# Hymba layer on one core: a third pair of gate-up group 1 made as seven products, and the token sums of pair 6 moved ahead of those of pair 5

## The chip, the cores and the metric

The kernel runs on 1 core of one Trainium2 chip. The metric is device time in microseconds (us), from the start to the end of the program on that core. Of each kernel there are several timed runs and one execution under the hardware profiler. Engines are named as in the profile: PE multiplies matrices, PEld loads their weights, DVE and ACT do elementwise work, POOL here mostly issues DMAs that add to memory, SP issues the other DMAs.

## The reference, cut to what matters

The layer is a feed-forward block, a mixer (a gated recurrence beside windowed attention) and a second feed-forward block, on 256 tokens of width 2048, all in float32. The change touches the gate-up product of both feed-forward blocks:

```python
def swiglu(x, w_gate_up, w_down):
    gate, up = jnp.split(x @ w_gate_up, 2, axis=-1)
    return (jax.nn.silu(gate) * up) @ w_down

ff = swiglu(rms_norm(x, pre_norm_ffn1[layer]), w_ffn1_gate_up[layer], w_ffn1_down[layer])
x = x + 0.5 * rms_norm(ff, post_norm_ffn1[layer])
...
ff = swiglu(rms_norm(x, pre_norm_ffn2[layer]), w_ffn2_gate_up[layer], w_ffn2_down[layer])
```

Here `w_gate_up` has 2048 rows and 2 x 5632 columns.

## The kernel before, in words

**Precision.** Every float32 operand is kept as two parts, a rounded `h` (cast by ACT) and the rest `l` (subtracted by DVE, `split_act`, L175 to L177). Each product is three matmuls: high by high, high by low, low by high (`three`, L435 to L447; the matmul is L441).

**Tiling of gate-up.** The columns are worked in 11 groups (0 to 10) of 512 gate and 512 up columns. In a group the 2048 rows of weights are 8 pairs (0 to 7) of two 128-row blocks. For one pair, the 256 tokens (two halves) by two row blocks by two column blocks form a 2 x 2 by 2 x 2 block product into four result banks `c[m][n]`. There are two ways to do it:

- a **plain** pair (`plain`, L450): eight block products, 24 matmuls of 512 columns. Its weights, 128 x 2048, come in one raw tile and are split in two halves: per half one ACT cast and one DVE subtraction (`split_half`, L168).
- a **seven** pair (`products`, L485): seven block products of sums, 21 matmuls, some into four more banks `p`. Its left sides are sums of the token blocks (made once by `sums_in`, L1023). Its right sides are sums of weight blocks: `prepare` (L903) splits the first block b11 (a 128 x 512 cast and subtraction) and lets POOL issue a DMA that adds 512 KB of weights onto the raw tile (L910). Later `splits` (L917) makes two 128 x 512 sums on DVE (L924, L925) and three half splits instead of two.

**The end of a group.** `boundary` (L1111) folds the `p` banks into the `c` banks by one ACT copy (L1122) and eight DVE additions (L1123 to L1133). Between them in the text, and waiting for them by bank, stand the 24 matmuls of pair 7, sorted by bank: (0,0) wants L1123, (1,0) wants L1126, (0,1) wants L1130, (1,1) wants L1133. Then follow the splits of pair 0 of the next group, and `units` (L1043): the gating of the finished group, which `first_pairs` (L1137) runs between the first pairs of the next.

**Order of the work.** From L1175 the order on every engine is the one written out by hand (`manual_schedule`): `first_pairs` for pairs 0 and 1, `pair_ahead` (L1156) for pairs 2 to 5, each of which first splits the weights of pair u + 1, then issues the products of pair u, then makes the last half split of u + 1; then pair 6 and the boundary. An engine does its instructions strictly in that order. Five `h` and five `l` buffers for halves go round (L44, L45), so ACT can cast a half only when PE has done with the half five places before. Weights come in five raw tiles; when a raw tile has been split, SP issues the next load (`load_next`, L894) in the order of a list that `plan` (L879) makes: by group and pair, with seven pairs moved forward by `PREPARED`.

**Which pairs are seven.** `MIXED_IN` is (2, 4, 5, 6). Groups 2 to 10 do these four as seven; group 1 does (2, 4); group 0 none. The token sums of pairs 2 and 4 are made in group 0 (L1105); those of pairs 5 and 6 in group 1, in `pair_ahead`, after pairs 4 and 5 (L1167). In `begin` (L413) the set of seven pairs of a group is read off as those pairs whose token sums exist; it sets how many matmuls each bank is to see.

Of the kernel before, what the change touches and what calls it, by code (L numbers as in the profile page):

```python
# [37 lines left out]
def hymba_layer_kernel(  # L38
# [37 lines left out]
    def nm(s):  # L76
        uid[0] += 1
        return f"{s}_{uid[0]}"

    def pa():  # L80
        return psum.tile([P, 512], F32, tag="pa", name=nm("pa"))

    def pb():
        return psum.tile([P, 512], F32, tag="pb", name=nm("pb"))
# [90 lines left out]
    def split_act(hi, lo, src):  # L175
        nc.scalar.copy(hi, src)  # L176
        nc.vector.tensor_tensor(lo, src, hi.bitcast(F32), ALU.subtract)  # L177
# [154 lines left out]
    class LeadN:  # L332


        def __init__(self, w, c0, slot):
            self.w, self.c0, self.slot = w, c0, slot
# [56 lines left out]
    def sums_of(u, w):  # L393

        nc.vector.tensor_tensor(
            w[:, S3::2, :], u[:, 0, :].rearrange("p (m t) -> p m t", m=2), u[:, :, P:T], ALU.subtract
        )
        nc.vector.tensor_tensor(w[:, S2, :], w[:, S1, :], u[:, 0, 0:P], ALU.subtract)
        nc.vector.tensor_tensor(w[:, S4, :], u[:, 1, 0:P], w[:, S2, :], ALU.add)
        return w  # L400

    class Blocks:
# [5 lines left out]
        rooms = 4  # L408

        def __init__(self, tiles, sums):  # L410
            self.tiles, self.sums = tiles, sums

        def begin(self, order, c=None):  # L413

            self.order, self.pos, self.seen = order, 0, {}
            self.c = c or [[pa(), pa()], [pb(), pb()]]
            self.p = None
            self.mixed = {u for u in order if u in self.sums}
            at = [i for i, u in enumerate(order) if u in self.mixed]
            some = len(at)  # L420
            plain = len(order) - some
            self.after = at[-1] + 1 if at else len(order) - 1

            self.within = bool(at) and self.after >= len(order) - 2

            self.rest = 6 * (len(order) - self.after - 1)
            self.of = {}
            for i in range(4):
                self.of["p", i] = 3 * some
                self.of["c", i // 2, i % 2] = 6 * plain + (3 * some if i < 3 else 0)  # L430
# [414 lines left out]
    NG = DFF // 512  # L845
    NU = DFF // 256
    LATE = 8

    MIXED_IN = (2, 4, 5, 6)
    PREPARED = {2: -0.5, 4: 0.5, 5: 1.5, 6: 3.5}  # L850
    AWAY = 8
    MIXED = range(0, 20, 2)
# [5 lines left out]
    class Gated(Blocks):  # L858
# [6 lines left out]

        def group(self, g, c=None):
            self.g = g
            self.begin(range(KT // 2), c)
            if g:
                self.rest = 6 if g < NG - 1 else 0  # L870
# [7 lines left out]

        def plan(self):  # L879

            self.here = {g: MIXED_IN if g > 1 else MIXED_IN[:2] for g in range(1, NG)}
            wanted = []
            for g in range(1, NG):
                for u in range(KT // 2):
                    before = PREPARED[u] if u in self.here[g] else u
                    wanted.append((g * KT // 2 + before, g, u))
            self.wanted = [at[1:] for at in sorted(wanted)]
            self.raws, self.firsts, self.split_of = {}, {}, {}
            for pool, n in ((rawp, 3), (self.room, 2)):
                for _ in range(n):  # L890
                    raw = pool.tile([P, 2048], F32, tag="raw", name=nm("raw"), bufs=n)
                    self.load_next(raw)
# [88 lines left out]
    def ffn(gated, w_dn, post_gain, again, gain=None, lead=None, aside=None):  # L981

        with ExitStack() as st:
# [6 lines left out]
            hts, sums, away = [], {}, {}  # L990
            where_X_was = []

            def room_for(tag):
                return work.tile([P, 512], F32, tag=tag, name=nm(tag))
# [21 lines left out]
            def even(u):  # L1016

                x = gated.tiles[u].rearrange("p k i t -> p (k i) t")
                nc.vector.tensor_tensor(
                    x, x.bitcast(F32), R[:, None, :].to_broadcast([P, 4, T]), ALU.mult  # L1020
                )

            def sums_in(u):  # L1023
                x = gated.tiles[u].bitcast(F32)
                whole = room_for("z").rearrange("p (k t) -> p k t", k=2)
                nc.vector.tensor_tensor(whole, x[:, :, 0, :], x[:, :, 1, :], ALU.add)
                ws = sums_of(whole, room_for("s").rearrange("p (j t) -> p j t", j=4))
                apart = u == MIXED_IN[1]
                w = (gated.room if apart else work).tile(
                    [P, 4, 2, P], F32R, tag="sp", name=nm("xs"), bufs=1 if apart else 3  # L1030
                )
                split_act(w[:, :, 0, :], w[:, :, 1, :], ws)
                gated.sums[u] = w

            def put_away(u):
                away[u] = dram.tile([P, 1024], F32, tag=f"ht{u}", name=nm("away"))
                nc.sync.dma_start(away[u], hts[u].bitcast(F32).rearrange("p k i t -> p (k i t)"))
# [54 lines left out]
            def some(steps, n):  # L1092
                for _ in range(n):
                    next(steps)
# [3 lines left out]
            for u in range(gated.pos, KT // 2):  # L1098
# [4 lines left out]
                for done in {4: (0, 1, 2), 5: (3, 4), 6: (5, 6), 7: (7,)}.get(u, ()):  # L1103
                    even(done)
                    if done in MIXED_IN[:2]:  # L1105
                        sums_in(done)
# [30 lines left out]
            def first_pairs(g, waiting):  # L1137

                gated.group(g)
                some(waiting, 1)  # L1140
                gated.prepare(g, MIXED_IN[1])
                some(waiting, 1)
                ahead = gated.splits(g, 1)
                some(ahead, 2)
                gated.prepare(g, MIXED_IN[2])
                for one in gated.take(g, 0):
# [9 lines left out]
            def pair_ahead(g, u):  # L1156

                ahead = gated.splits(g, u + 1)
                next(ahead)
                if u + 1 == MIXED_IN[1]:  # L1160
                    gated.prepare(g, MIXED_IN[3])
                next(ahead)
                for one in gated.take(g, u):
                    one()
                for _ in ahead:
                    pass
                if g == 1 and u in (4, 5):  # L1167
                    sums_in(MIXED_IN[u - 2])
                if u == 5 and 1 < g <= AWAY // 2 + 1:
                    put_away(2 * g - 4)  # L1170
                    put_away(2 * g - 3)
# [3 lines left out]
            with tc.manual_schedule():  # L1175
                gated.prepare(1, MIXED_IN[0])
                some(gated.splits(1, 0), 2)
                for g in range(1, NG):
                    first_pairs(g, waiting)
                    for u in range(2, last - 1):  # L1180
                        pair_ahead(g, u)
                    if g < NG - 1:
                        ahead = gated.splits(g, last)
                        some(ahead, 2)
                        gated.prepare(g + 1, MIXED_IN[0])
                        for one in gated.take(g, last - 1):
                            one()
                        boundary(g)
                        waiting = units(gated.c, rest)
                        some(waiting, 2)  # L1190
# [185 lines left out]
    with ExitStack() as s2:  # L1376
# [227 lines left out]
        def gates(half):  # L1604

            sl = [pa(), pa()]
            for _ in proj_N_pieces(w_in, 4096 + half * 512, 512, xt, sl):
                side_step()
            g = mid.tile([P, 2, 512], F32, tag="g", name=nm("g"))
            for m in range(2):  # L1610
                by = rs2[:, m : m + 1]
                nc.scalar.activation(g[:, m, :], sl[m], AF.Sigmoid, scale=by)
                nc.vector.scalar_tensor_tensor(g[:, m, :], sl[m], by, g[:, m, :], ALU.mult, ALU.mult)
            return g
# [129 lines left out]
        for hp in range(4):  # L1744
            zf = headpair(2048 + hp * 256, "zf")
            if hp == 1:
                g = gates(0)
# [18 lines left out]
        g = gates(1)  # L1766
# [94 lines left out]
```

## Time and profile before

| | us |
|---|---|
| median of 3 runs (lowest to highest) | 1833.95 (1833.39 to 1834.18) |
| the profiled execution, its own time | 1832.88 |
| its span, first to last instruction | 1831.1 |
| PE busy in the span | 1814.2 (99%) |
| DVE busy in the span | 1627.3 (89%) |
| ACT busy in the span | 1129.4 (62%) |

The profiled execution lies 1.07 us below the median of the runs, and 1.78 us of its time lie outside the span. A busy PE is counted with modelled ends that overlap, so how dense the matmuls are is read from their starts. In rows of the timeline the first number is the start in us from the beginning of the span and the second the duration; a number in brackets is idle time just before, with what ended it. In rows of windows follow, for each engine, busy us and instructions.

### The profile page before, as it was taken

Reading aid. Unit: us, or ns where it says so; the run is one execution under the profiler, and the core shown is the slowest. Engines: PE = TensorE matmul, PEld = TensorE weight load, DVE = VectorE, ACT = ScalarE, POOL = GpSimd, SP = SyncE. Lnnn points to the kernel's source line nnn. Section 1 sums busy time; section 2 is a strip of 40 time slices with the busy share of each in tenths; the row PEclk is TensorE's granted clock in tenths of the full one; section 3 lists DMA queues with packets and bytes.
Section 4 is the critical chain, followed back from the end, with each engine's and each line's share of the span. In section 5 each row is a group of like instructions: output and inputs, shape, how many; then the busy total and the mean of one; then the engine's idle time right before and its main releaser. Section 6 shows DMA issues by size and latency. Waiting matters only on the chain.

```text
span 1831.1 us, 23305 instructions
## 1 busy us (share of the span) xinstructions
PE 1814.2 (99%) x8438; PEld 1504.0 (82%) x8438; DVE 1627.3 (89%) x2071; ACT 1129.4 (62%) x1492; POOL 114.4 (6%) x115
## 2 busy tenths in 40 slices
PE   9999999999999999999999999999999999999998
PEld 6888888888887888888888888788888888888886
DVE  7999999999999998477787798899999999999897
ACT  7565666665655666476587556556666666565563
POOL 1011111111000000000000000001111111000000
PEclk9999999999999999999999999999999999999999
DMA  8789999998665566555454456789998998855565
GB/s 301 230 234 283 278 280 253 251 266 241 249 226 197 195 253 216 203 175 178 165 173 150 161 208 249 223 243 267 280 277 267 252 251 251 268 218 207 193 231 185
DMA packets 200020, 422.42 MB, mean 231 GB/s; under 512 B 10984, under 2 KB 45888, under 8 KB 199136
## 3 DMA queue, kind: packets, MB, share of 16 engines
q1 hardware_dynamic: 178880, 380.95, 59.6%
q0 software_dynamic: 21024, 39.99, 12.7%
q8 instruction: 66, 1.08, 0.2%
q14 instruction: 50, 0.41, 0.1%
HBM read 408.29 MB, written 12.60 MB: 230 GB/s over the span
## 4 chain that ended last, share of the span: by engine, by line
PE 87%; DVE 5%; ACT 3%; DMA 3%; issue 2%; POOL 0%; SPq 0%; DVEq 0%; ACTq 0%; POOLq 0%
PE pa L441 37%; PE pb L441 33%; PE pa L309 5%; DVE l L177 3%; PE pa L314 3%; DMA raw<-in_w_ffn_gate_up_dram 2%; PE pa L364 2%; PE pa L362 2%; PE pa L363 2%; ACT h L176 1%; PE pa L1074 1%; PE pb L1074 1%; PE pb L1582 0%; PE pb L1556 0%; PE pb L1660 0%
## 5 line engine op out<-in xcount | busy, mean ns | idle before, releaser
L176 ACT CAST h<-raw 128x1024 fp32r<-128x1024 f32 (+1 forms) x861 | 846.9, 1013 | 448.6 <-PE pb L441 131.9
L177 DVE TENSOR_TENSOR l<-raw,h 128x1024 fp32r<-128x1024 f32 (+1 forms) x861 | 983.1, 1171 | 118.3 <-ACT h L176 83.8
L441 PE MATMUL pa<-h,xt 128*128 128x512 f32 x1104 | 387.2, 392 | 0.1
L441 PE MATMUL pb<-h,xt 128*128 128x512 f32 x952 | 339.7, 391 | 0.4 <-DVE pb L1126 0.4
L441 PEld LDWEIGHTS pa<-h,xt 128*128 128x128 f32 x1104 | 207.2, 188 | 43.9 <-DVE xt L232 0.6
L441 PE MATMUL pa<-l,xt 128*128 128x512 f32 x552 | 215.7, 391 | 0.2 <-DVE l L177 0.2
L441 PEld LDWEIGHTS pb<-h,xt 128*128 128x128 f32 x952 | 178.6, 188 | 43.2 <-DVE pb L1133 3.5
L441 PE MATMUL pb<-l,xt 128*128 128x512 f32 x476 | 185.6, 390 | 0.0
L441 PE MATMUL pb<-h,ht 128*128 128x512 f32 x464 | 163.8, 390 | 0.0
L441 PE MATMUL pa<-h,ht 128*128 128x512 f32 x464 | 163.7, 391 | 0.0
L910 POOL DMA_DIRECT2D raw<-in_w_ffn_gate_up_dram x76 | 92.0, 1211 | 737.0 <-DVE l L177 638.8
L309 PE MATMUL pa<-xt,h 128*128 128x512 f32 x512 | 124.5, 393 | 0.2 <-ACT h L176 0.2
L441 PEld LDWEIGHTS pa<-l,xt 128*128 128x128 f32 x552 | 103.7, 188 | 21.4 <-DVE l L177 1.4
L309 PEld LDWEIGHTS pa<-xt,h 128*128 128x128 f32 x512 | 93.8, 188 | 18.6 <-ACT h L176 0.6
L441 PE MATMUL pa<-h,xs 128*128 128x512 f32 x304 | 108.5, 389 | 0.0
L441 PE MATMUL pb<-h,xs 128*128 128x512 f32 x304 | 105.9, 389 | 0.0
L441 PEld LDWEIGHTS pb<-l,xt 128*128 128x128 f32 x476 | 89.4, 188 | 17.2
L441 PEld LDWEIGHTS pa<-h,ht 128*128 128x128 f32 x464 | 87.7, 189 | 18.4
L441 PEld LDWEIGHTS pb<-h,ht 128*128 128x128 f32 x464 | 87.3, 188 | 18.1
L441 PE MATMUL pa<-l,ht 128*128 128x512 f32 x232 | 90.9, 392 | 0.0
L441 PE MATMUL pb<-l,ht 128*128 128x512 f32 x232 | 90.5, 390 | 0.0
L314 PE MATMUL pa<-xt,l 128*128 128x256 f32 x512 | 69.1, 285 | 0.0
(289 smaller groups left out, 2516.9 us busy)
## 6 DMA issues: line engine op xcount, KB each, us to landing
raw<-in_w_ffn_gate_up_dram SPq DMA_DIRECT2D x350, 512.0 KB, 6.1
raw<-in_w_ffn_down_dram SPq DMA_DIRECT2D x88, 1024.0 KB, 5.3
raw<-in_w_mix_in_dram SPq DMA_DIRECT2D x52, 1024.0 KB, 4.9
raw<-in_w_ffn_gate_up_dram POOLq DMA_DIRECT2D x76, 512.0 KB, 8.8
raw<-in_w_mix_out_dram SPq DMA_DIRECT2D x16, 1024.0 KB, 5.0
away<-ht SPq DMA_DIRECT2D x16, 512.0 KB, 6.9
ht<-away SPq DMA_DIRECT2D x16, 512.0 KB, 7.8
pg<-in_post_norm_ffn_dram SPq DMA_DIRECT2D x4, 512.0 KB, 6.7
```

Of the source, the lines that this page charges most:

```text
L176: nc.scalar.copy(hi, src)
L177: nc.vector.tensor_tensor(lo, src, hi.bitcast(F32), ALU.subtract)
L309: nc.tensor.matmul(slot[f], weights(hs, kk, f), xcol(xt, k), start=(k == 0), stop=(k == KT - 1))
L314: nc.tensor.matmul(slot[f][:, 0:T], weights(ls, kk, f), xcol(xt, kh * 8 + kk, 0), start=False, stop=False,)
L362: nc.tensor.matmul(dst, xh, h[:, o : o + n], start=(k == 0), stop=False)
L363: nc.tensor.matmul(dst, xh, l[:, o : o + n], start=False, stop=False)
L364: nc.tensor.matmul(dst, xl, h[:, o : o + n], start=False, stop=(k == KT - 1))
L441: nc.tensor.matmul(self.bank(at), lhs, rhs, start=(n == 1), stop=n in (ends, self.of[at]), skip_group_check=n > ends,)
L910: nc.gpsimd.dma_start(raw[:, 0:1024].rearrange("p (k c) -> p k c", k=2), self.source(u, g)[:, :, 1], accum_op=ALU.add,)
L1074: nc.tensor.transpose(bank[:, o : o + P], zs[m][:, k * P : (k + 1) * P], ident)
```

## The change

Group 1 does three pairs as seven products, (2, 4, 6). For that the token sums of pair 6 are made after pair 3, and those of pair 5 (wanted from group 2 on) after pair 5, both in group 1. The set of seven pairs is now taken from the plan (`here`) and no longer from the sums that exist. In `plan`, pair 6 of group 1 is now placed at 3.5 by `PREPARED`, so its weights are loaded ahead of those of pair 5. Both feed-forward blocks run this code.

```diff
-            self.tiles, self.sums = tiles, sums
+            self.tiles, self.sums, self.summed = tiles, sums, sums
...
-            self.mixed = {u for u in order if u in self.sums}
+            self.mixed = {u for u in order if u in self.summed}
...
     MIXED_IN = (2, 4, 5, 6)
+    MIXED_FIRST = (2, 4, 6)
     PREPARED = {2: -0.5, 4: 0.5, 5: 1.5, 6: 3.5}
...
         def group(self, g, c=None):
             self.g = g
+            self.summed = self.here[g] if g else ()
             self.begin(range(KT // 2), c)
...
-            self.here = {g: MIXED_IN if g > 1 else MIXED_IN[:2] for g in range(1, NG)}
+            self.here = {g: MIXED_IN if g > 1 else MIXED_FIRST for g in range(1, NG)}
...
-                if g == 1 and u in (4, 5):
-                    sums_in(MIXED_IN[u - 2])
+                if g == 1 and u in (3, 5):
+                    sums_in(6 if u == 3 else 5)
```

## The prediction

> **What bounds the kernel now.** First the page, then the windows between the transposes of one group and the next, in both feed-forward blocks (group 1, then group 2, of each).
>
> ```profile
> PE 1814.2 (99%) x8438; PEld 1504.0 (82%) x8438; DVE 1627.3 (89%) x2071; ACT 1129.4 (62%) x1492; POOL 114.4 (6%) x115
> ```
>
> ```profile
> 62.51:106.19 43.68, 43.48 (x195) 35.58 (x194) 40.11 (x53) 24.80 (x30) 2.50 (x3) 1.00 0.79 240
> 106.19:147.99 41.80, 41.80 (x189) 34.50 (x188) 39.82 (x49) 26.18 (x30) 4.81 (x4) 1.00 0.93 276
> ...
> 1177.99:1223.07 45.08, 43.95 (x195) 35.66 (x195) 42.06 (x54) 24.64 (x30) 3.65 (x3) 1.00 0.71 213
> 1223.07:1264.86 41.79, 41.79 (x189) 34.47 (x188) 39.82 (x49) 26.21 (x30) 4.84 (x4) 1.00 0.93 275
> ```
>
> PE is the bound over the whole, but DVE is close behind: in group 2 it is busy 39.82 of 41.80 us. Group 1 shows PE short of its window, so there it waits. The PE timeline shows where: the starts of pair 6, of pair 7, of pair 7's banks (1,0) and (1,1), and of the next group, then the like in the second block.
>
> ```profile
> 89.24 0.39 PE L441 MATMUL pa<-h,xt 128*128 128x512 f32 x1
> ...
> 94.68 0.39 PE L441 MATMUL pa<-h,xt 128*128 128x512 f32 x1
> ...
> 96.41 0.50 PE L441 MATMUL pb<-h,xt 128*128 128x512 f32 x1 [0.20 <-DVE pb L1126]
> ...
> 99.29 0.46 PE L441 MATMUL pb<-h,xt 128*128 128x512 f32 x1
> ...
> 100.75 0.39 PE L441 MATMUL pa<-h,xt 128*128 128x512 f32 x1
> ```
>
> ```profile
> 1211.58 0.39 PE L441 MATMUL pa<-h,xt 128*128 128x512 f32 x1
> ...
> 1213.31 0.50 PE L441 MATMUL pb<-h,xt 128*128 128x512 f32 x1 [0.20 <-DVE pb L1126]
> ...
> 1216.18 0.48 PE L441 MATMUL pb<-h,xt 128*128 128x512 f32 x1
> ```
>
> Pair 6 is 24 matmuls in 94.68 - 89.24 = 5.44 us: 0.2267 us each. Bank (1,0) should start six matmuls after 94.68, at 96.04, and starts at 96.41, just after a fold addition. So at the end of group 1 DVE, not PE, already sets the pace. Now DVE around it:
>
> ```profile
> 93.54 0.69 DVE L1123 TENSOR_TENSOR pa<-pa,z 128x512 f32<-128x512 f32 x1
> ...
> 95.65 0.70 DVE L1126 TENSOR_TENSOR pb<-pb,z 128x512 f32<-128x512 f32 x1
> ...
> 98.50 0.70 DVE L1133 TENSOR_TENSOR pb<-pb,s 128x512 f32<-128x512 f32 x1
> ```
>
> ```profile
> 1210.44 0.69 DVE L1123 TENSOR_TENSOR pa<-pa,z 128x512 f32<-128x512 f32 x1
> ...
> 1215.40 0.70 DVE L1133 TENSOR_TENSOR pb<-pb,s 128x512 f32<-128x512 f32 x1
> ```
>
> The last fold addition ends at 98.50 + 0.70 = 99.20 and bank (1,1) starts at 99.29; in the second block 1216.10 and 1216.18. The end of group 1 is tied to L1133, and what is tied to L1133 is what I have to move.
>
> **What the change takes from PE.** Pair 6 goes from 24 to 21 matmuls: 3 x 0.2267 = 0.68 us in each block, 1.36 us in all. It is worth that only if DVE is no later.
>
> **What it adds to DVE, per block.** One subtraction for b11, two sums, one more half split. Their price is read start to start:
>
> ```profile
> 60.40 0.68 DVE L177 TENSOR_TENSOR l<-raw,h 128x512 fp32r<-128x512 f32 x1
> 61.00 0.74 DVE L1054 SCALAR_TENSOR_TENSOR s<-pb,scales,s 128x512 f32<-128x512 f32 x1
> ...
> 65.18 0.69 DVE L924 TENSOR_TENSOR raw<-raw 128x512 f32<-128x512 f32 x1
> 65.91 0.69 DVE L925 TENSOR_TENSOR raw<-raw 128x512 f32<-128x512 f32 x1
> 66.52 1.22 DVE L177 TENSOR_TENSOR l<-raw,h 128x1024 fp32r<-128x1024 f32 x1
> ...
> 69.84 4.62 DVE L177 TENSOR_TENSOR l<-raw,h 128x1024 fp32r<-128x1024 f32 x4
> 74.50 0.69 DVE L924 TENSOR_TENSOR raw<-raw 128x512 f32<-128x512 f32 x1
> ...
> 75.84 3.64 DVE L177 TENSOR_TENSOR l<-raw,h 128x1024 fp32r<-128x1024 f32 x3
> 80.37 1.22 DVE L177 TENSOR_TENSOR l<-raw,h 128x1024 fp32r<-128x1024 f32 x1 [0.90 <-ACT h L176]
> 81.51 0.68 DVE L1026 TENSOR_TENSOR z<-xt 128x512 f32<-128x512 f32 x1
> ...
> 83.99 0.69 DVE L177 TENSOR_TENSOR xs<-s,xs 128x512 fp32r<-128x512 f32 x1 [0.69 <-ACT xs L176]
> 84.95 2.36 DVE L177 TENSOR_TENSOR l<-raw,h 128x1024 fp32r<-128x1024 f32 x2 [0.26 <-ACT h L176]
> ```
>
> The subtraction takes 61.00 - 60.40 = 0.60 us. A half split takes (4.62 - 1.22) / 3 = 1.13. The two sums take 66.52 - 65.18 = 1.34, and the first starts 74.50 - (69.84 + 4 x 1.13) = 0.14 later than a dense queue would. Together 0.60 + 1.34 + 0.14 + 1.13 = 3.21 us.
>
> **What it moves.** The token sums hold DVE from 81.51 to 84.95, 3.44 us, of which 0.69 + 0.26 us wait for ACT, whose cast of the next half stands behind its cast of the sums. There are two such sets in group 1 before and after, so moving them adds nothing in itself. But the first set, and the new subtraction, now come ahead of the splits of pair 5, where DVE has its only idle time: 0.90 us at 80.37, and about 0.15 us inside the three halves from 75.84 (3.64 where three dense ones take 1.22 + 2 x 1.13 = 3.48). There it waited for a buffer that PE had not done with. That idle time is filled. In the second block it is less:
>
> ```profile
> 1193.29 3.64 DVE L177 TENSOR_TENSOR l<-raw,h 128x1024 fp32r<-128x1024 f32 x3
> 1197.28 1.23 DVE L177 TENSOR_TENSOR l<-raw,h 128x1024 fp32r<-128x1024 f32 x1 [0.35 <-ACT h L176]
> ```
>
> So the folds come later by 3.21 - 0.90 - 0.15 = **2.16 us** in the first block and by 3.21 - 0.35 - 0.15 = **2.71 us** in the second. L1133 then ends at 101.36 and 1218.81, the last bank of group 1 starts as much later, and what stands behind keeps its distance to L1133. Sum: 4.87 us. The 1.36 us of PE are not subtracted: PE only comes to the boundary earlier and waits longer. Groups 2 to 9 do not give it back, because PE runs through them without a gap (41.80 us each).
>
> **What lies beside.** ACT gets a 512-wide and a 1024-wide cast more; it is busy 24.80 of 43.68 us in group 1, so they cost nothing unless it falls behind DVE. The first half of pair 5, which ended at 75.84 + 3.64 = 79.48, comes later by 0.60 + 3.44 - 0.15 = 3.89 us and ends at 83.37; PE starts pair 5 at 89.24 - 5.44 = 83.80. That cover is 0.4 us; if it fails PE waits there instead, and the fold is no later. SP loads pair 6 one place sooner and pair 5 one place later, both freed before 65 us and wanted after 72. POOL issues one more adding DMA per block, behind nothing: between its issues lie tens of us.
>
> **A stall long enough to slow PE.** In the first block PE now reaches pair 7 at 94.68 - 0.68 = 94.00 and may start when L1123 ends, at 94.23 + 2.16 = 96.39, plus 0.06 (96.41 against the end of L1126 at 96.35): a stall of 2.45 us. In the second it is 1210.90 to 1213.90, 3.0 us. Before bank (1,0) come 0.6 us more. The trace shows what a like stall does:
>
> ```profile
> 558.20:561.62 3.42, 1.38 (x6) 0.91 (x6) 3.42 (x5) 3.02 (x4) 0.00 (x0) 1.00 0.00 0
> 561.62:565.03 3.41, 3.41 (x10) 2.63 (x9) 3.41 (x5) 1.58 (x2) 0.00 (x0) 0.50 0.91 317
> 565.03:568.44 3.41, 3.41 (x17) 2.81 (x16) 3.37 (x5) 2.11 (x2) 0.00 (x0) 1.00 0.75 300
> ...
> 1176.02:1179.43 3.41, 2.48 (x13) 1.68 (x12) 2.25 (x4) 2.63 (x4) 0.25 (x1) 1.00 0.09 36
> ```
>
> After 3.41 us with 6 matmuls the granted clock is 0.50 for 3.41 us, with 10 matmuls where 17 stand otherwise; after 3.41 us with 13 it stays 1.00. Six matmuls leave 3.41 - 6 x 0.2267 = 2.05 us idle. If such windows lie anywhere in time, a stall s holds 2.05 us of one with a chance of (3.41 + s - 4.10) / 3.41: 0.52 and 0.68. So one drop in the two blocks is likeliest, none about 0.15, two about 0.35. Its price: up to 7 x 0.2267 = 1.6 us, but bank (1,0) waits in any case, and the last bank waits for L1133. With the drop from 97.4 on, bank (1,0) starts at 98.56 and takes 6 x 0.45 us for most of its length, ending near 101.0 where it would be 100.0; the last bank starts near 102.3 and not at 101.45. That is 0.9 us; an earlier drop gives 0.5, a later one 1.4. I take 0.9.
>
> The Trainium skill, "TensorE: Matmul & The Clock Gate", section "Part 1: The HAM clock gate", has the clock fall to half after at least one idle window of about 3.4 us. By that rule neither stall would slow PE and the sum would be 4.87 us (rival 1). The trace disagrees in part: its drop at 561.62 came after a window with 6 matmuls in it.
>
> **Forecast.** The profiled execution would go from 1832.88 to 1832.88 + 4.87 + 0.9 = 1838.65; the median of the runs lies 1.07 higher, so 1839.7.
>
> **Rivals.**
> (1) Late folds, no drop of the clock: 1833.95 + 4.87 = 1838.8. It speaks for it that where between 6 and 13 matmuls the drop sets in isn't shown.
> (2) Faster: DVE isn't the bound, its queue between 75.84 and 93.54 being held back by buffers that PE frees. Then PE alone counts: 1.36 us less, and of the waits in group 1 (0.37 + 0.1 us per block) nearly all go: 1831.6. It decides if 3.21 + 0.68 = 3.9 us of what looks like DVE work were waiting; the rows show 1.05 and 0.50 us, and twice 0.95 for ACT. Against it speak too the two PE waits that DVE ends now.
> (3) Half of it: the 0.95 us behind each set of token sums shrink, because in the new places ACT is ahead. Up to 1.9 us per block less if all four go; with half gone 1839.7 - 1.9 - 0.9 = 1836.9. Against it: ACT's order is fixed, and its cast of the next half stays behind that of the sums.
> (4) Worse: the adding DMA is late.
>
> ```profile
> DMA to landing us min/median/max: 5.6/8.8/10.7
> ```
>
> It is issued when the new subtraction ends, near 76.5, and the first sum of pair 6 is due at 75.84 + 0.60 + 2 x 1.13 + 3.44 + 3 x 1.13 + 0.14 = 85.7. At the median it lands at 85.3, at the longest 1.5 us late: up to 3 us in both blocks, 1842.7.
> (5) Pair 6 stays plain: 1834. The plan, the loads and the bank counts all read the new tuple, so next to nothing.
>
> **Chances.** Forecast 0.58 (one or two drops: 1839.2 to 1841); rival 1 0.16; rival 2 0.06; rival 3 0.10; rival 4 0.10; rival 5 none worth a number. The range runs from 1836.7 to 1841.9: it takes in the forecast, rival 1, most of rival 3 and the nearer half of rival 4. A measurement here can tell about 0.2%, 3.7 us, from no change: slower 0.84 (forecast, 1, 4), same 0.10 (rival 3), faster 0.06.
>
> **What would show it.** Right: 8432 matmuls on PE; L1123 of group 1 near 93.54 + 2.16 = 95.7 in the first block and near 1210.44 + 2.16 + 2.71 = 1215.3 in the second (later by what a drop of the clock costs ahead of it); PE idle 2 to 3 us ahead of pair 7 of group 1, released by DVE; no DVE wait of 0.90 us ahead of pair 5; groups 2 to 9 at 41.80 us; a clock of 0.50 just behind one of the stalls, or none for rival 1. Wrong: a wait of DVE at L924 for a DMA (rival 4), or PE reaching pair 7 with DVE already there (rival 2).

## The result and the profile after

The changed kernel takes 1836.73 us (median of 22 runs, 1835.32 to 1839.15), the kernel before, timed beside it, 1832.89 us (22 runs, 1830.26 to 1834.63). The ratio is 1.0023, with a 95% interval of 1.0017 to 1.0029: **slower** by some 4.2 us (3.1 to 5.3).

Lines L1122 to L1133 of the kernel before are L1124 to L1135 in the changed one. First the page, then the windows of group 1 in both blocks (us, then busy us and instructions of PE, PEld, DVE, ACT and POOL, the granted clock, DMA share and GB/s).

```profile
PE 1813.9 (99%) x8432; PEld 1505.0 (82%) x8432; DVE 1633.8 (89%) x2079; ACT 1135.2 (62%) x1496; POOL 116.8 (6%) x117
```

```profile
63.41:109.29 45.88, 43.11 (x193) 34.88 (x191) 43.13 (x57) 26.40 (x32) 3.67 (x4) 1.00 0.83 239
...
1179.31:1227.86 48.55, 44.80 (x191) 36.31 (x192) 45.81 (x59) 26.14 (x32) 5.07 (x5) 0.96 0.76 209
```

PE has its six matmuls fewer. Group 1 went from 43.68 to 45.88 us and from 45.08 to 48.55 us. In the first block PE is busy no longer than before, and DVE is busy 3.0 us longer. Now PE around pair 7 of group 1: the last matmul of pair 6, then the first of the banks.

```profile
94.67 0.39 PE L441 MATMUL pa<-h,xs 128*128 128x512 f32 x1
97.36 0.50 PE L441 MATMUL pa<-h,xt 128*128 128x512 f32 x1 [2.30 <-DVE pa L1125]
...
99.48 0.50 PE L441 MATMUL pb<-h,xt 128*128 128x512 f32 x1 [0.47 <-DVE pb L1128]
...
102.37 0.46 PE L441 MATMUL pb<-h,xt 128*128 128x512 f32 x1
...
103.83 0.39 PE L441 MATMUL pa<-h,xt 128*128 128x512 f32 x1
```

```profile
1212.05 0.39 PE L441 MATMUL pa<-h,xs 128*128 128x512 f32 x1
1215.26 0.79 PE L441 MATMUL pa<-h,xt 128*128 128x512 f32 x1 [2.82 <-DVE pa L1125]
...
1217.98 0.63 PE L441 MATMUL pb<-h,xt 128*128 128x512 f32 x1
...
1221.05 0.39 PE L441 MATMUL pb<-h,xt 128*128 128x512 f32 x1
```

PE should go on 0.23 us after 94.67 and stands until 97.36: 2.46 us, and 2.98 us in the second block. What ends both stalls is the first fold addition. DVE in group 1 of the first block:

```profile
76.70 2.96 DVE L177 TENSOR_TENSOR l<-raw,h 128x512 fp32r<-128x512 f32 x3
79.58 0.68 DVE L1028 TENSOR_TENSOR z<-xt 128x512 f32<-128x512 f32 x1
...
83.01 3.50 DVE L177 TENSOR_TENSOR l<-raw,h 128x1024 fp32r<-128x1024 f32 x3 [0.26 <-ACT h L176]
86.54 0.69 DVE L926 TENSOR_TENSOR raw<-raw 128x512 f32<-128x512 f32 x1
...
87.87 2.50 DVE L177 TENSOR_TENSOR l<-raw,h 128x1024 fp32r<-128x1024 f32 x2
90.29 0.68 DVE L1028 TENSOR_TENSOR z<-xt 128x512 f32<-128x512 f32 x1
...
93.73 2.96 DVE L177 TENSOR_TENSOR l<-raw,h 128x1024 fp32r<-128x1024 f32 x3 [0.26 <-ACT h L176]
96.61 0.69 DVE L1125 TENSOR_TENSOR pa<-pa,z 128x512 f32<-128x512 f32 x1
...
101.58 0.70 DVE L1135 TENSOR_TENSOR pb<-pb,s 128x512 f32<-128x512 f32 x1
```

The token sums of pair 6 (L1028 at 79.58) stand where DVE waited 0.90 us before, and the wait is gone. From 76.70 on DVE's waits are the two for ACT inside each set of token sums, and some 0.15 us inside the two halves from 87.87 (2.50 us where two dense ones take 1.22 + 1.13 = 2.35). The first fold addition starts at 96.61; counted from the transposes of this group (63.41 here, 62.51 before) that is 95.71, where 93.54 stood: 2.17 us later. In the second block L1125 starts at 1214.52; this group began 1.32 us later than before, so it is 2.76 us later than 1210.44.

```profile
1214.52 0.69 DVE L1125 TENSOR_TENSOR pa<-pa,z 128x512 f32<-128x512 f32 x1
...
1219.48 0.70 DVE L1135 TENSOR_TENSOR pb<-pb,s 128x512 f32<-128x512 f32 x1
```

The clock in the 3.41 us windows around the two stalls:

```profile
95.71:99.12 3.41, 1.65 (x6) 1.05 (x6) 3.27 (x6) 1.83 (x2) 1.21 (x1) 1.00 0.75 219
99.12:102.53 3.41, 3.05 (x13) 2.30 (x14) 3.24 (x6) 0.82 (x2) 0.00 (x0) 1.00 1.04 210
1211.87:1215.28 3.41, 0.59 (x4) 0.17 (x2) 3.41 (x5) 3.41 (x5) 0.03 (x1) 1.00 0.41 96
1215.28:1218.69 3.41, 3.41 (x8) 2.73 (x9) 3.17 (x5) 0.16 (x1) 1.18 (x1) 0.50 0.98 288
```

The second stall was followed by a window at half the clock, the first was not. Groups 2 to 9 take 41.8 us each, as before.

### The profile page after: what moved, and what is told of

Same layout as the page of the kernel before. It is cut to its first block, busy times and chain, and to the rows that moved or that the text cites. A ratio compares the mean times of both kernels' runs of the same rounds, so it can differ in the third digit from the quotient of the medians.

```text
span 1834.7 us, 23314 instructions
## 1 busy us (share of the span) xinstructions
PE 1813.9 (99%) x8432; PEld 1505.0 (82%) x8432; DVE 1633.8 (89%) x2079; ACT 1135.2 (62%) x1496; POOL 116.8 (6%) x117
## 4 chain that ended last, share of the span: by engine, by line
PE 90%; DVE 5%; ACT 3%; DMA 1%; issue 1%; POOL 0%; DVEq 0%; SPq 0%; ACTq 0%; POOLq 0%
PE pa L441 39%; PE pb L441 34%; PE pa L309 5%; PE pa L314 3%; DVE l L177 2%; PE pa L364 2%; PE pa L363 2%; PE pa L362 2%; ACT h L176 1%; DMA raw<-in_w_ffn_down_dram 1%; PE pa L1076 1%; PE pb L1076 1%; DMA raw<-in_w_ffn_gate_up_dram 0%; PE pb L1584 0%; PE pb L1558 0%
```

## Experiments

**Theory**: the work queued on DVE in group 1 sets when the folds of that group end, PE waits for them, and a long enough wait halves PE's clock for a while. **Rivals**: the order of the token sums, the order of the loads, or the seven pair itself (its adding DMA, its bank order) does it. Later a second question came up: what is given back outside group 1.

**1. The order of the token sums alone.**

```diff
-    MIXED_FIRST = (2, 4, 6)
+    MIXED_FIRST = (2, 4)
```

> Group 1 keeps two seven pairs (2, 4); only the order of the token sums is new (pair 6 after pair 3, pair 5 after pair 5). Theory (DVE's queue sets when the folds of group 1 come, and the sums in their new place fill the idle time ahead of pair 5): the folds come 1.05 us sooner in the first block and 0.50 us in the second, PE waits 0.1 us or less at the boundary, and the time is 0.6 to 1.1 us below the kernel before. Rival (the moved sums delay pair 5 and cost by themselves): PE waits at pair 5 and the time is 1 us or more above the kernel before.

1831.1 us against 1832.18, ratio 0.9993 (0.9984 to 1.0002). Group 1 in the windows:

```profile
63.88:107.01 43.13, 43.13 (x196) 35.69 (x194) 40.15 (x53) 24.93 (x30) 2.51 (x3) 1.00 0.81 239
1177.28:1221.95 44.67, 43.74 (x194) 35.66 (x195) 41.99 (x55) 24.54 (x30) 3.65 (x3) 1.00 0.73 214
```

That is 0.55 and 0.41 us less than before; PE has no gap left in the first. The timing alone can't tell so little, the windows can. The moved sums cost nothing, they gain a little.

**2. Four seven pairs in group 1.**

```diff
-    MIXED_FIRST = (2, 4, 6)
+    MIXED_FIRST = (2, 4, 5, 6)
...
-                if g == 1 and u in (3, 5):
-                    sums_in(6 if u == 3 else 5)
+                if g == 1 and u in (3, 4):
+                    sums_in(5 if u == 3 else 6)
```

> Group 1 makes four pairs (2, 4, 5, 6) as seven products, the token sums of pair 5 after pair 3 and those of pair 6 after pair 4. Theory (DVE bound, no idle time left to fill): 3.21 us more per block than the changed kernel, less at most 0.3 us of small waits, so 6 to 6.4 us above it and 10.5 to 12 us above the kernel before, with PE stalls of about 6 us ahead of pair 7 and a clock of 0.50 after both. Rival (the loss of the change comes from the order or the loads, not from DVE work): 1.4 us less than the changed kernel, PE's 6 matmuls.

1840.81 us, ratio 1.0051 (1.0037 to 1.0065). The windows of group 1 are 49.31 and 51.15 us, together 6.0 us more than in the changed kernel (45.88 and 48.55): the theory, not the rival. But the stall came elsewhere, in pieces, and the total rose by only 4 to 5 us over the changed kernel (ratios 1.0051 and 1.0023 to 1.0026). PE's waits in the first block:

```profile
86.83 0.50 PE L441 MATMUL pa<-l,xs 128*128 128x512 f32 x1 [0.36 <-DVE l L177]
91.42 0.50 PE L441 MATMUL pa<-h,xt 128*128 128x512 f32 x1 [1.08 <-ACT h L176]
92.68 0.50 PE L441 MATMUL pa<-l,xt 128*128 128x512 f32 x1 [0.76 <-DVE l L177]
95.27 0.80 PE L441 MATMUL pa<-l,xs 128*128 128x512 f32 x1 [1.62 <-DVE l L177]
```

With so much queued on DVE, PE already waits for the splits of pairs 5 and 6, and the clock fell to 0.50 for 6.83 us in both blocks (in the second also for 3.41 us at the start of the group, from 1182.84).

**3. PE kept busy while it waits.**

```diff
+    zeros = stat.tile([P, 208], BF16, tag="line", name="line", bufs=1)
+    nc.vector.memset(zeros, 0.0)
...
+                if g == 1:
+                    for _ in range(25):
+                        nc.tensor.matmul(
+                            c[1][1][:, 0:208], zeros[:, 0:P], zeros, start=False, stop=True, skip_group_check=True
+                        )
                 bank(0, 0)
                 bank(1, 0)
```

> The changed kernel, with 25 matmuls of zeros (208 columns, added to the bank (1,1)) ahead of pair 7 of group 1, where PE otherwise stands still: the result is the same. Theory (a stall of 2.45 or 3.0 us makes the clock drop in more than half of the executions, 0.9 us each): no granted clock of 0.50 near either boundary, the folds as late as in the changed kernel, and a median 0.8 to 1.3 us below the changed kernel. Rival (the drop costs nothing, since the last bank waits for DVE anyway): the same time as the changed kernel within 0.3 us.

1836.03 us, ratio 1.0020 (1.0011 to 1.0028). The matmuls of zeros fill the stall:

```profile
94.78 0.39 PE L442 MATMUL pa<-h,xs 128*128 128x512 f32 x1
95.00 2.40 PE L1132 MATMUL pb<-line 128*128 128x208 bf16 x25
97.49 0.50 PE L442 MATMUL pa<-h,xt 128*128 128x512 f32 x1
```

The clock stayed at 1.00 in both blocks, and group 1 took 46.00 and 47.94 us: the cost without a drop. The times don't show the 0.8 to 1.3 us that were expected: this run lies 3.85 us above the kernel before that was timed beside it (1832.18), the changed kernel 3.84 us above its own in the result above and 3.96 in run 7 below, and the intervals of the ratios overlap. The windows show a part of it: both groups 1 together take 93.94 us, where the three profiled executions of the changed kernel (the result above, runs 7 and 8 below) took 94.43, 95.59 and 94.80.

**4. The token sums' additions on POOL.**

```diff
...
+                add = nc.gpsimd.tensor_tensor
+                add(t, x[:, :, 0, :], x[:, :, 1, :], ALU.add)
...
+                if g == 1 and u in (2, 4):
+                    raw_sums(6 if u == 2 else 5)
+                if g == 1 and u in (3, 5):
+                    split_sums(6 if u == 3 else 5)
```

> The changed kernel, with the additions of both token sums of group 1 done by POOL, one pair ahead of their split; DVE keeps only the split's subtraction. Theory (DVE bound): DVE is freed of 2 x 2.8 us per block, more than the 3.21 us that the third seven pair adds; no PE stall at the boundary of group 1, group 1 at about 42.5 us in the first block, and 2.0 to 2.6 us below the kernel before. Rival (POOL's additions hinder DVE, or come late): a PE or DVE wait behind POOL, and a time at or above that of the kernel before.

1833.51 us, ratio 1.0008 (0.9999 to 1.0017): the expected gain didn't come. Group 1 is 44.71 and 46.79 us, better than the changed kernel, but PE still waits for the fold. DVE first, then POOL, at the same time:

```profile
70.76 6.52 DVE L177 TENSOR_TENSOR l<-raw,h 128x1024 fp32r<-128x1024 f32 x4
...
78.66 4.61 DVE L177 TENSOR_TENSOR l<-raw,h 128x512 fp32r<-128x512 f32 x3
...
83.79 4.29 DVE L177 TENSOR_TENSOR l<-raw,h 128x1024 fp32r<-128x1024 f32 x3
```

```profile
70.43 1.28 POOL L1030 TENSOR_TENSOR z<-xt 128x512 f32<-128x512 f32 x1 [6.91 <-DVE sums L399]
71.79 1.61 POOL L1031 TENSOR_TENSOR s<-z 128x256 f32<-128x256 f32 x1
73.47 1.33 POOL L1032 TENSOR_TENSOR s<-s,z 128x128 f32<-128x128 f32 x1
74.88 1.32 POOL L1033 TENSOR_TENSOR s<-z,s 128x128 f32<-128x128 f32 x1
```

The four half splits take 4.62 us in the kernel before; the two groups of three, beside the second set of additions, take 2.96 and 3.50 in the changed kernel. So DVE is slower by 1.90 + 1.65 + 0.79 = 4.3 us, of the 2 x 2.8 us that were taken from it: most of that work comes back as slower work. This run can't serve as the proof that DVE binds; the next one does.

**5. The token sums of pair 5 left out.**

```diff
-                if g == 1 and u in (3, 5):
-                    sums_in(6 if u == 3 else 5)
+                if g == 1 and u == 3:
+                    sums_in(6)
+                    gated.sums[5] = gated.sums[6]
```

> The changed kernel without the token sums of pair 5: groups 2 to 10 use those of pair 6 in their place, so a part of the computation is left out. Theory (the amount of DVE work in group 1 sets when the folds come, whatever work it is): 3.44 us less of DVE per block brings the folds to 1.28 us before their place in the kernel before (first block) and 0.73 us (second); no PE stall, group 1 at 42.4 to 42.6 us in the first block, the time 2.0 to 2.6 us below the kernel before. Rival (the third seven pair itself holds PE up, by its loads, its adding DMA or its bank order): a PE stall stays at pair 6 or 7, and the time stays 2 us or more above the kernel before.

1828.94 us against 1832.91, ratio 0.9977 (0.9968 to 0.9987): 4 us less, where 2.0 to 2.6 was expected. Both groups 1 together give 88.76 - 86.92 = 1.84 us of it; the rest lies outside them and belongs to runs 9 to 11.

```profile
63.40:105.86 42.46, 42.46 (x192) 35.13 (x191) 40.77 (x52) 26.07 (x31) 3.65 (x4) 1.00 0.90 258
1175.79:1220.25 44.46, 43.39 (x191) 34.96 (x192) 42.76 (x54) 25.67 (x31) 4.85 (x4) 1.00 0.82 227
```

```profile
93.21 0.69 DVE L1125 TENSOR_TENSOR pa<-pa,z 128x512 f32<-128x512 f32 x1
```

With three seven pairs and 3.44 us less of DVE, PE runs through group 1 of the first block without a gap: 42.46 us, 1.22 less than before (0.68 of PE work and the old waits). In the second block no wait for a fold is left either; the 1.07 us in which PE isn't busy lie at the start of the group, where its transposes wait 0.93 us for DVE's L1056, as they did in the kernel before (L1054, 0.93 us). So neither the seven pair's loads, its adding DMA nor its bank order holds PE up; what DVE's queue holds in group 1 does. Of the 3.44 us taken from that queue 0.95 us were waits for ACT, whose cast went too; the run doesn't tell the two apart. The fold is where it was expected: DVE's L1125 starts at 93.21 in a group begun 0.89 us later, so 1.22 us ahead of its old place (1.28 expected).

**6. The token sums of pair 5 in group 2.**

```diff
-                if g == 1 and u in (3, 5):
-                    sums_in(6 if u == 3 else 5)
+                if (g, u) in ((1, 3), (2, 3)):
+                    sums_in(6 if g == 1 else 5)
```

> The changed kernel with the token sums of pair 5 made in group 2, after its pair 3, where they are first used. Theory (DVE bound by group, about 1.1 us of idle time per group): the stall of group 1 goes, group 2 gets one instead: 3.44 us more of DVE less some 1.1 us of idle time and less 0.5 to 1 us of lead, so 1.3 to 1.9 us. Per block 1.2 us less in group 1 and 1.3 to 1.9 us more in group 2: from the time of the kernel before to 1.5 us above it, 2.5 to 4 us below the changed kernel. Rival (the folds of group 1 are late for another reason than the sums): group 1 as in the changed kernel.

1834.36 us against 1832.91, ratio 1.0005 (0.9996 to 1.0014). Groups 1 and 2 of the first block, then of the second:

```profile
63.38:105.84 42.46, 42.46 (x192) 35.09 (x191) 40.76 (x52) 26.18 (x31) 3.70 (x4) 1.00 0.89 253
105.84:149.95 44.11, 42.46 (x189) 34.31 (x188) 42.02 (x54) 25.95 (x31) 4.81 (x4) 1.00 0.91 261
1178.82:1223.23 44.41, 43.35 (x192) 34.95 (x192) 42.72 (x54) 25.70 (x31) 4.85 (x4) 1.00 0.81 227
1223.23:1267.36 44.13, 42.47 (x189) 34.30 (x188) 42.04 (x54) 26.07 (x31) 4.84 (x4) 1.00 0.90 260
```

Group 1 is as in run 5. Group 2 pays 2.3 us over its 41.8 in each block, where 1.3 to 1.9 was expected: about 1.1 us of its 3.44 us are hidden. By that sum nothing is left of the lead that DVE had at the end of group 1; where it went isn't shown.

**7 and 8. The changed kernel twice more.**

> The changed kernel once more, beside the others. Theory: 4 to 6 us above the kernel before; PE idle 2.45 and 3.0 us ahead of pair 7 of group 1; a granted clock of 0.50 behind one of the two stalls more often than not. Rival (the time measured first was low or high by chance): a ratio outside 1.0017 to 1.0029.

> The changed kernel, one look, for the clock alone: the same stalls of 2.45 and 3.0 us in the same places, and at each of the two a drop to 0.50 or none, by where the stall falls in the 3.41 us windows. If the drop comes when a window holds 2.05 us of idle time or more, the place of the windows in this execution tells beforehand which of the two it is.

Run 7: 1836.87 us against 1832.91, ratio 1.0026 (1.0017 to 1.0036). Its clock fell behind both stalls, and group 1 took 46.58 and 49.01 us. Run 8, a single execution (1836.34 us), had a drop behind the second alone, 45.89 and 48.91 us. The windows of run 7:

```profile
95.00:98.41 3.41, 1.12 (x5) 0.64 (x4) 3.41 (x5) 3.28 (x5) 0.43 (x1) 1.00 0.47 126
98.41:101.82 3.41, 3.41 (x9) 2.60 (x8) 3.13 (x6) 0.00 (x0) 0.78 (x1) 0.50 1.04 289
```

The windows lie otherwise in each of these executions, and in these six stalls the idle time that falls into one window decides. Adding up the gaps between PE's starts in each 3.41 us window: no drop after 1.76 us of idle time (run 8, first block) or 2.03 us (changed kernel, first block), a drop after 2.18 (run 7, second block), 2.31 (run 8, second), 2.54 (run 7, first) and 2.98 us (changed kernel, second).

**9 to 11. The order of the loads.** Outside group 1 the changed kernel is faster than the one before: the medians lie 3.84 us apart, while both groups 1 together cost 5.67, 6.83 and 6.04 us more in the three profiled executions of the changed kernel. In the profile its span less the two windows is 1834.7 - 45.88 - 48.55 = 1740.3 us, where it was 1831.1 - 43.68 - 45.08 = 1742.3. Run 1 shows 1743.1, run 5 1739.9. What the changed kernel and run 5 share is that pair 6 is loaded ahead of pair 5 (and the third seven pair). Three kernels change that order alone: run 9 is the changed kernel with the old order (first edit), run 10 the kernel before with the new one (second edit), run 11 is run 1 with the new one (second edit).

```diff
-                    before = PREPARED[u] if u in self.here[g] else u
+                    before = PREPARED[u] if u in self.here[g] and (g, u) != (1, 6) else u
```

```diff
-                    before = PREPARED[u] if u in self.here[g] else u
+                    before = PREPARED[u] if u in self.here[g] or (g, u) == (1, 6) else u
```

> The changed kernel, but in group 1 the weights of pair 6 are loaded behind those of pair 5, as in the kernel before. Theory (the changed order of the two loads moves every later raw tile by one place, so that the first loads of the down product are issued at other times, and DVE enters the down product further ahead; that gives back about 2 us of the 5.7 to 6.8 us that group 1 costs): group 1 as in the changed kernel, and the rest of the program (span less the two group 1's) at 1742 to 1744 us, where the changed kernel shows 1739.8 to 1741.2; about 2 us above the changed kernel. Rival (what is given back has to do with the third seven pair or is chance): the rest stays at 1740 us and the time is that of the changed kernel.

> The kernel before, but in group 1 the weights of pair 6 are loaded ahead of those of pair 5. Theory (order of the loads gives back about 2 us): both group 1's as in the kernel before (43.7 and 45.1 us), the second load of the down product issued 17 us and not 22.5 us before the end of group 10, the rest at 1739.5 to 1741 us; 1.5 to 2.5 us below the kernel before. Rival: no difference.

> Two seven pairs in group 1 with the new order of the token sums and the new order of the loads, that is the change without its third seven pair. Theory: the 1 us of the order of the sums and the 2 us of the loads add up, 2.5 to 3.5 us below the kernel before and 7 to 8 us below the changed kernel. Rival: no more than the order of the sums alone, 1 us.

| kernel | loads of 5 and 6 | seven pairs | ratio (interval) | rest, us | PE's waits in the down products, us |
|---|---|---|---|---|---|
| before | old | 2 | 1 | 1742.3 | 2.80 |
| run 1 | old | 2 | 0.9993 (0.9984 to 1.0002) | 1743.1 | 3.52 |
| run 9 | old | 3 | 1.0031 (1.0019 to 1.0044) | 1741.9 | 2.26 |
| changed | new | 3 | 1.0023 (1.0017 to 1.0029) | 1740.3 | 0.94 |
| run 7 | new | 3 | 1.0026 (1.0017 to 1.0036) | 1741.2 | 1.18 |
| run 10 | new | 2 | 0.9994 (0.9985 to 1.0003) | 1741.4 | 2.08 |
| run 11 | new | 2 | 0.9986 (0.9977 to 0.9995) | 1740.8 | 2.16 |

The rest is the span less both windows of group 1, of one profiled execution each. It is 1741.9 to 1743.1 us with the old order and 1740.3 to 1741.4 with the new (runs 2, 3, 4, 5 and 8, of the new order too: 1738.2 to 1740.1). But run 9 and run 10 lie only 0.5 us apart, three executions of the changed kernel (with run 8) spread over 1.4 us, and the 1742.3 us of the kernel before hold the drop of the clock at 561.62 that the prediction shows, up to 1.6 us by its sum, and that no other kernel of the table had there. Run 10 gained 0.7 us where 1.5 to 2.5 was expected, run 11 1.6 where 2.5 to 3.5 was, and between the pairs the intervals overlap.

The down products are where PE's waits differ. PE in the first of them, the kernel before and then the changed one:

```profile
559.51 0.49 PE L441 MATMUL pb<-h,sp 128*128 128x512 f32 x1 [1.27 <-ACT h L176]
560.77 0.50 PE L441 MATMUL pb<-l,sp 128*128 128x512 f32 x1 [0.77 <-DVE l L177]
```

```profile
562.35 0.50 PE L441 MATMUL pb<-l,sp 128*128 128x512 f32 x1 [0.76 <-DVE l L177]
```

The last column adds up such waits in both blocks. With the old order and two seven pairs they are 2.80 and 3.52 us; with the new order alone or the third seven pair alone 2.08 to 2.26; with both 0.94 and 1.18 (run 8: 0.90; run 2, with four seven pairs, 0.24). So what comes back can't be laid to the order of the loads alone: the third seven pair seems to have as large a part. The order moves the second and third load of the down product, issued 22.3 and 17.3 us ahead of the end of group 10 in place of 28.5 and 22.6 (first block); how that, or the third seven pair, shortens the waits isn't shown. This stays open: some two us come back outside group 1, and these runs don't show by what.

Run 9 shows something else well: neither stall was followed by a drop in it (2.03 and 2.05 us of idle time in the windows), so its group 1 is the price of DVE alone. (Its second window below begins and ends 0.4 us ahead of the transposes; from transposes to transposes it is as long.)

```profile
63.83:109.74 45.91, 43.10 (x192) 34.88 (x191) 43.17 (x57) 26.37 (x32) 3.70 (x4) 1.00 0.81 234
1180.04:1227.92 47.88, 43.29 (x190) 34.59 (x191) 45.14 (x59) 26.52 (x33) 4.85 (x4) 1.00 0.76 210
```

Run 11, with group 1 at 43.09 and 44.68 us and at 1830.39 us against 1831.99, is faster than both kernels: the change without its third seven pair.

## Why the prediction held, point by point

- **What bounds.** DVE's folds end group 1. Run 5 shows it: DVE work taken away, the third seven pair left, and PE has no gap. That it is the last fold, L1133, isn't shown: by the rows PE waits for the first ones (L1126 before, L1125 and L1128 behind the change) and runs without a gap from there, and in the first block the last bank starts 0.09 us after the last fold ends and at the same time just when PE is free. As all folds move together, the sum is the same. Where the clock is halved even that doesn't hold: in the second block of the changed kernel L1135 ends at 1219.48 + 0.70 = 1220.18, and the last bank starts at 1221.05, when PE gets to it.
- **The DVE term.** 2.16 and 2.71 us were predicted. Run 9, without a drop of the clock, has group 1 at 45.91 - 43.68 = 2.23 and 47.88 - 45.08 = 2.80 us over the kernel before. The four prices read start to start, and the 0.90 and 0.35 us of idle time that were to be filled, came out; of the small 0.15 us as much is left in the changed kernel, in another place.
- **The PE term.** Six matmuls went and gave nothing in the changed kernel, since the stall grew by as much: 2.46 and 2.98 us where 2.45 and 3.0 were predicted.
- **The clock.** One drop in two stalls was forecast; the four executions with these stalls (changed kernel, runs 7, 8 and 9) had one, two, one and none. The price was put at 0.9 us. In the first block run 7 stands 0.67 us above run 9; in the second the changed kernel, run 7 and run 8 stand 0.67, 1.13 and 1.03 us above it. The bound of 2.05 us of idle time, taken from a window with six matmuls, was close: in these runs a drop comes somewhere between 2.05 us (run 9, none) and 2.18 us (run 7). That it was close is luck: by the gaps between PE's starts the window at 558.20 was itself idle for 2.45 us. The Trainium skill, "TensorE: Matmul & The Clock Gate", section "Part 1: The HAM clock gate", has the clock fall after an idle window of about 3.4 us. The length of the window agrees; that all of it must be idle doesn't, by these numbers.
- **What came out smaller.** The forecast was 1839.7, the median 1836.73. Of the 2.97 us, 1.06 are the base: three runs of the kernel before had a median of 1833.95, 22 runs one of 1832.89. The other 1.9 us is the step "groups 2 to 9 do not give it back": true of these groups, but nothing was said of the down products behind them, and there PE waited 0.9 to 1.2 us where it had waited 2.8. The prediction put the new order of the loads at nothing because both were landed in time, and followed neither it nor the third seven pair beyond group 1; which of them gives the time back isn't shown. So the mechanism of group 1 came out, and its size; the total, 5.75 us forecast against the kernel before and 3.84 measured, came out a third smaller. The median lies only 0.03 us above the lower end of the stated range, 1836.7, and that end was drawn for rival 3, which didn't come: that it lies inside is in part luck.
- **The rivals.** "Late folds, no drop" is what the profiled execution of run 9 shows. "Faster" (rival 2) fell with the result and with run 5. "Half of it" (rival 3) asked that the waits behind the token sums shrink; they stayed at 0.69 and 0.26 us. A late adding DMA (rival 4) didn't show: no wait of DVE at L926, and in the first block only 0.65 us of idle time of ACT ended by a DMA onto the raw tile. "Pair 6 stays plain" (rival 5) fell with the 8432 matmuls.

## What to carry to other kernels

Where one engine is 99% busy, look at each stage for the engine that ends it: a product that saves the busy engine 0.68 us is a loss when it adds 3.2 us to an engine whose queue has 1 us to spare. Price such a step start to start in the trace, take off the idle time that it will fill, and follow the delay to the first instruction that waits. Then ask what the change does to the stages that come later, and whether the new stall is long enough to slow the clock.

## What the runs showed of the hardware beyond that

POOL's additions slow DVE. Four DVE subtractions of 128x1024 took 6.52 us with POOL adding beside them and 4.62 us without. The Trainium skill, "GPSIMD Engine Reference", section "1. Specifications", says that POOL shares its memory interfaces with DVE, with contention when a DVE instruction has two inputs in that memory; these subtractions do, and the trace agrees. POOL's additions beside DVE took no less for 128x128 (1.33 us, where DVE takes 0.29) than for 128x512 (1.28 us).
